# A hybrid decoder block on one core: stores requested by another engine, and the order of retention's statistics

## The chip, the cores and the metric

The kernel runs on one core of a Trainium2 chip. A core has five engines that run side by side, each through its own instructions in order: TensorE (PE: matmuls and transposes), VectorE (DVE), ScalarE (ACT), GpSimd (POOL) and SyncE (SP, which here only requests transfers). Transfers between HBM and the on-chip memory (SBUF) run on 16 DMA engines; a transfer starts when an engine's queue reaches its request, and an engine that requests one waits first, in order, until the data is ready and the place is free. PE's results go to a small memory of banks (PSUM), which ACT and DVE empty. The metric is the device time of one execution in microseconds, the median of several runs.

## The reference

One decoder layer on 1024 tokens of width 1024, in float32:

```python
xn = rmsnorm(x, norm1_g)
qa, ka, va, qr, kr, vr, gr, gate_a, gate_b = split(xn @ w_in)
o_a = mix over 3 dilations of softmax(norm(qa) @ norm(ka).T * s - slope * dist) @ va    # 12 heads of 128
o_r = retention(qr, kr, vr)                       # 4 heads, chunks of 128 tokens, a state of 256 x 512
o_r = head_groupnorm(o_r) * silu(gr)
y = sigmoid(gate_a) * (o_a @ w_proj_a) + sigmoid(gate_b) * (o_r @ w_proj_b)
x = x + y @ w_out
x = x + square(relu(rmsnorm(x, norm2_g) @ w_up)) @ w_down
```

Retention walks through the 8 chunks of a head: each chunk's output is a decayed product inside the chunk plus q times the state, and the state is then decayed and updated with the chunk's k and v. The group norm needs the mean and variance of the 512 outputs of each token and head.

## The kernel before, in words

Every float32 operand is split into a high and a low part (helper `split`, L459 to L466: ACT writes the high part, DVE the low part at L463), and a product is three matmuls of 128x128 by 128x512 (`Pipe.group`, L356). The large products use Strassen's scheme: seven quarter products N1 to N7 for each unit of 256 columns (`product`, L514 and on), whose partial results ACT and DVE combine (L533 to L547). PE's order is written out by hand: `manual_schedule` covers PE, and a `Pipe` drops other matmuls (attention, transposes) between the terms of a product, so many slots later. The other engines' instructions are ordered by a planner, by what its own model expects to be ready, unless the kernel pins one: `tc.keep_in_program_order(ins)` puts `ins` behind the instruction traced before it on the same engine. All pools use `reuse_waits="tile"`: a new tile waits for the tile whose place it takes.

The stages that matter, in order of time:

- **Input projection**, 36 units: 12 of attention's q and k, 8 of retention's output gate gr, 8 of the two mixing gates, 8 of retention's q and k. `result` (L1188) takes each quarter result: a gr quarter goes through sigmoid and a product into a tile `sg` (two buffers) and is stored in `sr_d` (L1206); the others are stored in `sg_d` and `rqk_d` (L1212), from `sg` or straight from the tile `u`.
- **Attention** is woven into the later units (`attend`, L989; `plan_core`). For each head it loads bias, qk, scales and values (L1052 to L1075), scales q and k on DVE (L1069), and works block by block: scores (L1005), exp, transposes (L1016), values (L1026). Two blocks share an `acc` tile of four buffers, which is stored in `acc_d` (L1031); `load_heads` (L581) reads it back to mix the three dilations.
- **Retention**, 4 heads of 8 chunks. `load_chunk` (L1294) brings q, k (L1302) and the silu gate (L1304) two chunks ahead. `decay` makes the inner scores and splits them and q; `output` makes the chunk's product, has ACT copy it (L1364), takes statistics on DVE (L1366, L1367), a power on POOL (L1369) and normalises (L1371); `update` renews the state (L1383); `turn_o` transposes the result (L1396), multiplies by the gate and, for the later half of the chunks, has POOL form the sums of Strassen's scheme (L1410 to L1413), which SP stores in `on_d` (L1391).
- **Projection of attention's output** (pa): 16 products; each is multiplied with a gate on DVE (L1465), put on a list by `leave` and stored in `pa_d` by `send` (L1263).
- **Projection of retention's output** (pb): 8 units in two rounds. A quarter result is gated and added on DVE (L1531); the first round's sums go to `pb_d` and four blocks of the second to `yl_d`, also by `send`. Gates and partial sums come in by `place` (L1250), which loads into the first free buffer of the list `spots`; `send` puts a stored buffer back on that list, and the next load into it waits for the store to land. The operands come from `on_d` (L1276) and are split.

Then follow the output projection, the second norm and the MLP, which the change does not touch. SP requests nearly all transfers of the kernel.

Of the kernel before, what the change touches and what calls it, by code (L numbers as in the profile page):

```python
# [10 lines left out]
F = mybir.dt.float32  # L11
# [6 lines left out]
P = 128  # L18
# [388 lines left out]
def hybrid_block(ctx: ExitStack, tc: tile.TileContext, a: dict, out: bass.AP):  # L407
# [158 lines left out]
    def tokens(rows, g, b):  # L566

        if g == 0:
            return rows[b * P:(b + 2) * P].rearrange("(k p) e -> p k e", k=2)
        if g == 1:  # L570
            return rows.rearrange("(k p r) e -> r p k e", k=2, r=4)[b // 2]
        return rows.rearrange("(p r) e -> p r e", r=8)[:, b:b + 2]
# [416 lines left out]
    def attend(n, b, bias, qk, V, acc, core):  # L989

        slot, g = heads[n]
        h = g * SLOTS + slot
        nk = 2 if has_prev(g, b) else 1
        w = nk * P
        st = {}
        pair, acc = acc, acc[:, b % 2]

        def scores():
            sp = tr.tile([P, 4, P], F, name="tr")[:, :nk].rearrange("p a b -> p (a b)")
            q = qk[b // 4][:, 0, b % 4 * P:b % 4 * P + P]  # L1000
            at = 0
            for c in range((b + 1 - nk) // 4, b // 4 + 1):
                n0, n1 = max(b + 1 - nk, 4 * c), min(b + 1, 4 * c + 4)
                to = slice(at, at + (n1 - n0) * P)
                nc.tensor.matmul(sp[:, to], q, qk[c][:, 1, (n0 - 4 * c) * P:(n1 - 4 * c) * P], start=True, stop=True)  # L1005
                at = to.stop
            s = st["p"] = core.tile([P, 2 * P], F, name="s", bufs=3)
            nc.vector.tensor_tensor_reduce(s[:, :w], sp, bias[:, -w:], op0=OP.add, op1=OP.min,
                                           scale=1.0, scalar=3.0e38, accum_out=acc[:, DH:DH + 1])
            nc.scalar.activation(s[:, :w], s[:, :w], AF.Exp, scale=-1.0, bias=acc[:, DH:DH + 1],  # L1010
                                 accum_out=acc[:, DH + 1:DH + 2])

        def turn(bank):
            tp = bank[:, 1:]
            for j in range(nk):
                nc.tensor.transpose(tp[:, j], st["p"][:, j * P:(j + 1) * P], ident)  # L1016

        def turned(bank):
            st["t"] = core.tile([P, 2, P], F, name="pT", bufs=2)
            nc.scalar.activation(st["t"][:, :nk], bank[:, 1:1 + nk], AF.Copy)  # L1020

        def values(bank):
            po = bank[:, 0]
            for j in range(nk):
                k = b + 1 - nk + j
                nc.tensor.matmul(po, st["t"][:, j], V[k // 2][:, k % 2], start=(j == 0), stop=(j == nk - 1))  # L1026

        def valued(bank):
            nc.scalar.activation(acc[:, :DH], bank[:, 0], AF.Copy)
            if b % 2:  # L1030
                nc.sync.dma_start(tokens(acc_d[:, h, :], g, b - 1), pair)  # L1031

        return scores, turn, turned, values, valued

# [100 lines left out]
    with ExitStack() as ph:  # L1135
# [52 lines left out]
        def result(j, f, cs, src):  # L1188
            if j < NA:
                i = cs.start // 512  # L1190
                r = strides(heads[j][1])
                sg = sgp.tile([P, 512], F, name="sg")
                nc.scalar.activation(sg.rearrange("p (r i) -> p r i", r=r), src.rearrange("p (i r) -> p r i", r=r),
                                     AF.Copy)
                to = qk_d[j, :, f].rearrange("p (r j i) -> j p r i", r=r, j=2)[i]
                src = sg.rearrange("p (r i) -> p r i", r=r)
                nc.sync.dma_start(to, src)
                square(j, f, i, sg)
                return
            n = j - NA  # L1200
            sg = src
            if n < 8:
                sg = sgp.tile([P, 512], F, name="sg")
                nc.scalar.activation(sg, src, AF.Sigmoid)
                nc.vector.tensor_tensor(sg, src, sg, op=OP.mult)
                nc.sync.dma_start(sr_d[2 * n + f, :, cs], sg)  # L1206
                return
            if src.space == PSUM:
                sg = sgp.tile([P, 512], F, name="sg")
                nc.scalar.activation(sg, src, AF.Copy)  # L1210
            n -= 8
            nc.sync.dma_start(sg_d[f, n, :, cs] if n < NG else rqk_d[(n - NG) // 2, (n - NG) % 2, f, :, cs], sg)  # L1212

        unit = {}
        NIN = NA + NG + NQ + 8
# [43 lines left out]
    def send():  # L1259

        while leaving:
            to, y = leaving.pop(0)
            nc.sync.dma_start(to, y)  # L1263
            spots.append(y)

    def sigmoid(x):
# [19 lines left out]
    with ExitStack() as ph:  # L1286
        comb, load = ExitStack(), ExitStack()
        pc = pool(comb, "pc", 2)
        p2 = pool(ret, "p22", 2, "right")
        p2b = pool(ph, "p22b", 2, "right")  # L1290

# [2 lines left out]
        def load_chunk(n):  # L1294

            if n >= RH * NT:
                return
            h, c = divmod(n, NT)
            ts = slice(c * P, (c + 1) * P)
            qk = [p2.tile([P, 2, P], F, name=x, bufs=3) for x in ("rqT", "rkT")]  # L1300
            for i in range(2):
                (nc.scalar if n == 1 else nc.sync).dma_start(qk[i], rqk_d[h, i, :, :, ts].rearrange("f p t -> p f t"))  # L1302
            sr = p2.tile([P, 4, P], F, name="sr", bufs=4)
            nc.sync.dma_start(sr, sr_d[4 * h:4 * h + 4, :, ts].rearrange("f p t -> p f t"))  # L1304
            ready[n] = (*qk, sr)

# [11 lines left out]
        for h in range(RH):  # L1318
# [4 lines left out]
            for c in range(NT):  # L1323
# [9 lines left out]
                def decay(c=c, h=h, it=it, qT=qT, kT=kT):  # L1333
                    sp = ms.tile([P, 512], F, name="ms")
                    for f in range(2):
                        nc.tensor.matmul(sp[:, :P], kT[:, f], qT[:, f], start=(f == 0), stop=(f == 1))  # L1336
                    sm = p2b.tile([P, P], F, name="sm")
                    nc.vector.tensor_tensor(sm, sp[:, :P], maskT[:, h, :], op=OP.mult)
                    it["s"] = p2.tile([P, P], R, name="smh", bufs=3), p2.tile([P, P], R, name="sml", bufs=3)
                    split(*it["s"], sm)  # L1340
                    if c > 0:
                        it["q"] = p2.tile([P, 2, P], R, name="qh", bufs=3), p2.tile([P, 2, P], R, name="ql", bufs=3)
                        split(*it["q"], qT)
                    if c < NT - 1:
                        pt = tr.tile([P, 4, P], F, name="tr")
                        for f in range(2):
                            nc.tensor.transpose(pt[:, f, :], kT[:, f], ident)
                        kzh = p2b.tile([P, 2, P], R, name="kzh", bufs=3)
                        kzl = p2b.tile([P, 2, P], R, name="kzl", bufs=3)
                        nc.scalar.activation(kzh, pt[:, :2], AF.Copy, scale=rc[:, 2, h:h + 1])  # L1350
                        nc.vector.scalar_tensor_tensor(kzl, pt[:, :2], rc[:, 2, h:h + 1], kzh.bitcast(F),
                                                       op0=OP.mult, op1=OP.subtract)
                        it["k"] = kzh, kzl

                def output(c=c, h=h, it=it, state=state):
                    po = ms.tile([P, 512], F, name="ms")
                    terms = [(*it["s"], *it["v"])]
                    if c > 0:
                        for f in range(2):
                            terms.append((it["q"][0][:, f, :], it["q"][1][:, f, :], state["h"][:, f, :],  # L1360
                                          state["l"][:, f, :]))
                    pipe.group(po, terms)
                    on = p2.tile([P, DV], F, name="on")
                    nc.scalar.activation(on, po, AF.Copy)  # L1364
                    st = p2.tile([P, 12], F, name="st")
                    nc.vector.bn_stats(st[:, 0:6], on)  # L1366
                    nc.vector.bn_aggr(st[:, 6:8], st[:, 0:6])  # L1367
                    nc.vector.tensor_scalar(st[:, 8:9], st[:, 7:8], rc[:, 1, h:h + 1], EPS, op0=OP.mult, op1=OP.add)
                    nc.gpsimd.tensor_tensor(st[:, 9:10], st[:, 8:9], half[:, 0:1], op=OP.pow)  # L1369
                    nc.vector.tensor_scalar(st[:, 10:11], st[:, 9:10], rc[:, 0, h:h + 1], None, op0=OP.mult)  # L1370
                    nc.vector.tensor_scalar(on, on, st[:, 6:7], st[:, 10:11], op0=OP.subtract, op1=OP.mult)  # L1371
                    it["o"] = on
# [629 lines left out]
```

## Time and profile before

| | before |
|---|---|
| timed runs, us | 2147.24 median of 3 (2146.48 to 2148.41) |
| the profiled execution, us | 2145.36 |
| its span, first to last instruction, us | 2143.5 |
| PE busy, us | 2132.2 |
| DVE, ACT, POOL busy, us | 1385.2, 1119.1, 312.1 |
| granted TensorE clock | 1.000 |

Rows of the profile name an engine, a line of the kernel (L1031), an operation and its tiles as out<-in. "PEld" is PE's weight load, which overlaps the matmuls; an engine with a q (SPq) is its queue of requests. A row of waits reads: who waited for whom, microseconds in total, how often, the longest. A row of a timeline reads: start, duration, engine, line, operation, and in brackets how long the engine had been idle and what ended that. A row of the chain of waits reads: start, duration, what. Matmuls overlap in this profile, and their ends are modelled.

### The profile page before, as it was taken

Reading aid. Unit: us, or ns where it says so; the run is one execution under the profiler, and the core shown is the slowest. Engines: PE = TensorE matmul, PEld = TensorE weight load, DVE = VectorE, ACT = ScalarE, POOL = GpSimd, SP = SyncE. Lnnn points to the kernel's source line nnn. Section 1 sums busy time; section 2 is a strip of 40 time slices with the busy share of each in tenths; the row PEclk is TensorE's granted clock in tenths of the full one; section 3 lists DMA queues with packets and bytes.
Section 4 is the critical chain, followed back from the end, with each engine's and each line's share of the span. In section 5 each row is a group of like instructions: output and inputs, shape, how many; then the busy total and the mean of one; then the engine's idle time right before and its main releaser. Section 6 shows DMA issues by size and latency. Waiting matters only on the chain.

```text
span 2143.5 us, 28506 instructions
## 1 busy us (share of the span) xinstructions
PE 2132.2 (99%) x9840; PEld 1752.5 (82%) x9840; DVE 1385.2 (65%) x2360; ACT 1119.1 (52%) x2154; POOL 312.1 (15%) x340
## 2 busy tenths in 40 slices
PE   9999999999999999999999999999999999999999
PEld 7887777888888888888888887888788888888887
DVE  7944434656556565657767777973865557788884
ACT  8534555434655454445545655542655555755552
POOL 1000000000000000003123110000000000777773
PEclk9999999999999999999999999999999999999999
DMA  9433333333667766765364498854354556645443
GB/s 331 152 113 98 108 104 103 104 134 134 194 197 216 210 197 192 221 192 163 104 177 128 150 307 294 305 196 142 105 168 140 159 157 200 217 156 195 155 143 108
DMA packets 297489, 368.24 MB, mean 172 GB/s; under 512 B 35249, under 2 KB 202609, under 8 KB 297089
## 3 DMA queue, kind: packets, MB, share of 16 engines
q1 hardware_dynamic: 296800, 366.16, 53.7%
q8 instruction: 77, 1.26, 0.3%
q14 instruction: 68, 0.55, 0.1%
q10 hardware_dynamic: 544, 0.26, 0.0%
HBM read 249.76 MB, written 116.59 MB: 171 GB/s over the span
## 4 chain that ended last, share of the span: by engine, by line
PE 89%; DVE 4%; DMA 2%; issue 2%; ACT 2%; POOL 1%; SPq 0%; POOLq 0%; DVEq 0%; ACTq 0%
PE mm L356 45%; PE ms L356 34%; PE ms L811 3%; PE tr L1026 1%; PE tr L1005 1%; PE mm L811 1%; DVE wl L463 1%; PE tr L1016 1%; PE tr L1396 1%; PE tr L1158 1%; PE ms L1336 1%; ACT wh L460 1%; DVE xl L463 1%; DVE raw L160 1%; DVE xn L1682 0%
## 5 line engine op out<-in xcount | busy, mean ns | idle before, releaser
L463 DVE TENSOR_TENSOR wl<-raw,wh 128x1024 fp32r<-128x1024 f32 (+1 forms) x301 | 333.7, 1110 | 388.9 <-ACT wh L460 387.8
L460 ACT ACTIVATE wh<-raw 128x1024 fp32r<-128x1024 f32 (+1 forms) x301 | 288.0, 959 | 290.5 <-PE ms L356 96.0
L356 PE MATMUL mm<-xh,wh 128*128 128x512 f32 x960 | 387.7, 404 | 0.6 <-ACT q L1718 0.4
L356 PE MATMUL mm<-xh,wl 128*128 128x512 f32 x960 | 374.9, 391 | 0.5 <-DVE wl L463 0.5
L356 PE MATMUL mm<-xl,wh 128*128 128x512 f32 x960 | 374.1, 390 | 0.3 <-DVE xl L463 0.3
L356 PE MATMUL ms<-xh,wh 128*128 128x512 f32 x784 | 317.6, 405 | 1.5 <-ACT u L541 1.5
L356 PE MATMUL ms<-xh,wl 128*128 128x512 f32 x784 | 306.2, 391 | 0.1
L356 PE MATMUL ms<-xl,wh 128*128 128x512 f32 x784 | 305.5, 390 | 0.0
L356 PEld LDWEIGHTS mm<-xh,wl 128*128 128x128 f32 x960 | 180.2, 188 | 40.0 <-DVE wl L463 1.2
L356 PEld LDWEIGHTS mm<-xh,wh 128*128 128x128 f32 x960 | 180.5, 188 | 35.4 <-ACT q L1718 0.8
L356 PEld LDWEIGHTS mm<-xl,wh 128*128 128x128 f32 x960 | 180.7, 188 | 34.8 <-DVE xl L463 0.7
L356 PE MATMUL mm<-wh,xh 128*128 128x512 f32 x474 | 192.1, 405 | 0.0
L356 PE MATMUL mm<-wh,xl 128*128 128x512 f32 x474 | 185.6, 392 | 0.0
L356 PE MATMUL mm<-wl,xh 128*128 128x512 f32 x474 | 184.7, 390 | 0.0
L356 PEld LDWEIGHTS ms<-xh,wh 128*128 128x128 f32 x784 | 147.4, 188 | 40.7 <-issue 10.1
L1369 POOL TENSOR_TENSOR st<-st,half 128x1 f32<-128x1 f32 x32 | 25.2, 788 | 1043.8 <-DMA at<-acc_d 886.5
L356 PEld LDWEIGHTS ms<-xh,wl 128*128 128x128 f32 x784 | 147.1, 188 | 32.3 <-DVE wl L463 0.5
L356 PEld LDWEIGHTS ms<-xl,wh 128*128 128x128 f32 x784 | 147.6, 188 | 27.3
L356 PEld LDWEIGHTS mm<-wh,xl 128*128 128x128 f32 x474 | 89.0, 188 | 19.8
L356 PEld LDWEIGHTS mm<-wl,xh 128*128 128x128 f32 x474 | 89.4, 189 | 16.3
L356 PEld LDWEIGHTS mm<-wh,xh 128*128 128x128 f32 x474 | 89.2, 188 | 16.2 <-ACT ms L1809 0.3
L160 DVE TENSOR_TENSOR raw<-raw 128x512 f32<-128x512 f32 x120 | 83.5, 696 | 1.9
(368 smaller groups left out, 3836.7 us busy)
## 6 DMA issues: line engine op xcount, KB each, us to landing
raw<-in_w_up SPq DMA_DIRECT2D x32, 512.0 KB
h_d<-s SPq DMA_DIRECT2D x64, 256.0 KB
raw<-in_w_down SPq DMA_DIRECT2D x30, 512.0 KB
xl<-on_d SPq DMA_DIRECT2D x28, 512.0 KB
raw<-in_w_aqk_q SPq DMA_DIRECT2D x24, 512.0 KB
qk_d<-sg SPq DMA_DIRECT2D x48, 256.0 KB
qk<-qk_d SPq DMA_DIRECT2D x24, 512.0 KB
rb<-rs_d SPq DMA_DIRECT2D x24, 512.0 KB
```

The source lines that it names most:

```text
L160: ins = self.nc.vector.tensor_tensor(x, x, y, op=OP.add)
L356: self.nc.tensor.matmul(ps, x, y, start=start, stop=stop, skip_group_check=not first)
L460: hi = nc.scalar.activation(dst_h, src, AF.Copy)
L463: lo = nc.vector.tensor_tensor(dst_l, src, dst_h.bitcast(F), op=OP.subtract)
L811: nc.tensor.matmul(pm, x, w, start=k == m == 0, stop=k == n - 1 and m == 2)
L1005: nc.tensor.matmul(sp[:, to], q, qk[c][:, 1, (n0 - 4 * c) * P:(n1 - 4 * c) * P], start=True, stop=True)
L1016: nc.tensor.transpose(tp[:, j], st["p"][:, j * P:(j + 1) * P], ident)
L1026: nc.tensor.matmul(po, st["t"][:, j], V[k // 2][:, k % 2], start=(j == 0), stop=(j == nk - 1))
L1158: nc.tensor.matmul(to[m:m + 32], pick[:, 31 - n:63 - n], x, start=n == 0, stop=n == HEADS - 1)
L1336: nc.tensor.matmul(sp[:, :P], kT[:, f], qT[:, f], start=(f == 0), stop=(f == 1))
L1369: nc.gpsimd.tensor_tensor(st[:, 9:10], st[:, 8:9], half[:, 0:1], op=OP.pow)
L1396: nc.tensor.transpose(pt[:, f, :], it["o"][:, f * P:(f + 1) * P], ident)
```

## The change

Four requests move from SP's queue to POOL's: the stores of the silu gates, of the mixing gates and retention's q and k (`result`), of attention's pairs (`valued`), and of the gated blocks (`send`). In retention the tiles of q, k and the silu gate get a pool of their own, opened ahead of the pool they were in, with the same number of buffers. The low part of q's split is pinned behind the DVE instruction traced before it, and so are the two statistics instructions.

```diff
         def valued(bank):
             nc.scalar.activation(acc[:, :DH], bank[:, 0], AF.Copy)
             if b % 2:
-                nc.sync.dma_start(tokens(acc_d[:, h, :], g, b - 1), pair)
+                nc.gpsimd.dma_start(tokens(acc_d[:, h, :], g, b - 1), pair)
...
-                nc.sync.dma_start(sr_d[2 * n + f, :, cs], sg)
+                nc.gpsimd.dma_start(sr_d[2 * n + f, :, cs], sg)
                 return
...
-            nc.sync.dma_start(sg_d[f, n, :, cs] if n < NG else rqk_d[(n - NG) // 2, (n - NG) % 2, f, :, cs], sg)
+            nc.gpsimd.dma_start(sg_d[f, n, :, cs] if n < NG else rqk_d[(n - NG) // 2, (n - NG) % 2, f, :, cs], sg)
...
         while leaving:
             to, y = leaving.pop(0)
-            nc.sync.dma_start(to, y)
+            nc.gpsimd.dma_start(to, y)
             spots.append(y)
...
         pc = pool(comb, "pc", 2)
+        p2a = pool(ret, "p22a", 3, "right")
         p2 = pool(ret, "p22", 2, "right")
...
-            qk = [p2.tile([P, 2, P], F, name=x, bufs=3) for x in ("rqT", "rkT")]
+            qk = [p2a.tile([P, 2, P], F, name=x) for x in ("rqT", "rkT")]
...
-            sr = p2.tile([P, 4, P], F, name="sr", bufs=4)
+            sr = p2a.tile([P, 4, P], F, name="sr", bufs=4)
...
-                        split(*it["q"], qT)
+                        split(*it["q"], qT, False, True)
...
-                    nc.vector.bn_stats(st[:, 0:6], on)
-                    nc.vector.bn_aggr(st[:, 6:8], st[:, 0:6])
+                    tc.keep_in_program_order(nc.vector.bn_stats(st[:, 0:6], on))
+                    tc.keep_in_program_order(nc.vector.bn_aggr(st[:, 6:8], st[:, 0:6]))
```

## The prediction

> **What bounds the kernel now.** I read the page first, then the stages, then what TensorE (PE) waits for, then the queue of SyncE (SP).
>
> ```profile
> span 2143.5 us, 28506 instructions
> ...
> PE 2132.2 (99%) x9840; PEld 1752.5 (82%) x9840; DVE 1385.2 (65%) x2360; ACT 1119.1 (52%) x2154; POOL 312.1 (15%) x340
> ```
>
> PE is busy in all but 11.3 us of the span (2143.5 - 2132.2). No store costs anything unless it makes PE late. The change touches five stages, in this order: the silu gates of the input projection; its last part with attention woven in; retention; the projection of attention's output (pa); the projection of retention's output (pb). Columns: span, then busy time of PE, PEld, DVE, ACT, POOL, granted clock, DMA share, GB/s.
>
> ```profile
> 360.00:546.00 186.00, 185.67 (x834) 151.54 (x833) 108.86 (x155) 91.80 (x139) 0.00 (x0) 1.00 0.39 130
> 546.00:913.00 367.00, 366.65 (x1874) 309.71 (x1873) 218.69 (x608) 187.10 (x525) 0.00 (x0) 1.00 0.66 203
> 913.00:1232.00 319.00, 317.63 (x1539) 262.71 (x1538) 229.12 (x518) 171.88 (x360) 67.28 (x84) 1.00 0.53 153
> 1232.00:1286.00 54.00, 53.95 (x240) 43.55 (x239) 39.95 (x57) 30.98 (x47) 9.11 (x13) 1.00 0.92 309
> 1286.00:1440.00 154.00, 152.23 (x668) 124.69 (x667) 129.59 (x172) 82.19 (x116) 0.00 (x0) 1.00 0.78 267
> ```
>
> Span less PE: 0.33 + 0.35 us in the two parts of the projection, 1.37 in retention, 0.05 in pa, 1.77 in pb; 3.87 us in all. The clock is 1.00 throughout, so throttling plays no part. GpSimd (POOL) does nothing at all in the projection and in most of pa and pb. PE's waits between 500 and 1400 us, with total, number and longest:
>
> ```profile
> PE ms L356 <- ACT u L541: 1.5, 2, 1.0
> PE tr L1396 <- DVE on L1371: 1.1, 3, 0.6
> PE tr L1005 <- DVE acc L1008: 0.4, 1, 0.4
> PE tr L1005 <- DVE qk L1069: 0.3, 1, 0.3
> ```
>
> Idle time understates a wait, because matmuls overlap. The rows around the longest one, in pb:
>
> ```profile
> 1320.67 0.39 PE L356 MATMUL mm<-xl,wh 128*128 128x512 f32 x1
> 1320.90 0.39 PE L356 MATMUL mm<-xh,wl 128*128 128x512 f32 x1
> 1322.30 0.50 PE L356 MATMUL ms<-xh,wh 128*128 128x512 f32 x1 [1.01 <-ACT u L541]
> ```
>
> Matmuls start 0.23 us apart, but each is shown for 0.39. The wait reads 1.01 us, and the start came 1.40 - 0.23 = 1.17 us late: 0.16 is hidden under each wait. I estimate ten waits in these stages (seven in the rows above, and shorter ones for the 0.57 us of idle time that these leave), so the change can return at most 3.87 + 10 x 0.16, about 5.4 us: about 1.0 in the projection, 2.1 in retention, 2.3 in pb. That is 0.25% of the kernel, the ceiling of what it aims at.
>
> **The moved stores, on SP's side.** By the loops, 180 requests change queue: 32 silu gates, 32 gates, 32 retention q and k, 48 attention pairs, 16 + 16 + 4 gated blocks. What SP loses in cost and in waits:
>
> ```profile
> L1206 SPq DMA_DIRECT2D sr_d<-sg x32: 319/326/877, 362.8 to 546.1; - x32
> ```
> ```profile
> SPq L1031 <- ACT acc L1029: 64.7, 24, 5.7
> ...
> SPq L1263 <- DVE s L1531: 21.7, 17, 3.4
> ```
>
> At the median 0.326 us, 180 requests are 59 us of SP's time, and the stores of pairs and blocks held SP another 64.7 + 21.7 = 86.4 us while it waited for ACT and DVE. Loads stand behind those waits. Only two places show PE paying for it. In attention:
>
> ```profile
> 822.94 0.37 SPq L1031 DMA_DIRECT2D acc_d<-acc  x1
> 823.40 0.53 SPq L1059 DMA_DIRECT2D qk<-qk_d  x1
> 824.03 0.55 SPq L1061 DMA_DIRECT2D rb<-rs_d  x1
> ```
> ```profile
> 830.65 0.75 DVE L1069 SCALAR_TENSOR_TENSOR qk<-qk,gqk,rb 128x512 f32<-128x512 f32 x1 [2.92 <-DMA rb<-rs_d]
> ```
>
> The loads of the next head leave right behind a pair's store; DVE then sits 2.92 us for them and PE is late for the score matmul behind it (the 0.4 row; 0.56 with the hidden part). Freed of the store, the loads can leave earlier, and 0.6 us is enough. The other wait of L1005 (0.3) has DVE's own queue ahead of it and may stay. I take -0.6; bounds 0 and -1.0.
>
> In pb:
>
> ```profile
> 1312.77 0.32 SPq L1263 DMA_DIRECT2D pb_d<-s  x1
> 1313.13 0.94 SPq L1276 DMA_DIRECT2D xl<-on_d  x2
> ```
> ```profile
> 1320.19 1.06 ACT L460 ACTIVATE xh<-xl 128x1024 fp32r<-128x1024 f32 x1 [0.38 <-DMA xl<-on_d]
> ```
>
> Two loads of 512 KB leave right after a store that waited for DVE; ACT, in order, waits for their landing (1320.19), evacuates u after it, and that is the 1.01 us above. Leaving 1.2 us earlier would erase it, if the DMA engines were free; at a share of 0.78 they are partly not. I take half of the 2.3: -1.2; bounds 0 and -2.3.
>
> **The same stores, on POOL's side.** No row shows a DMA request by POOL. From below a request costs SP's 0.326 us, from above POOL's longest neighbour here:
>
> ```profile
> 985.70 1.60 POOL L1411 TENSOR_TENSOR n<-onT,onE 128x256 f32<-128x256 f32 x1
> ```
>
> I take 1.0, nearer the middle since nothing tells: 180 us of an engine that is idle there, so 0 on the path. What covers it is the slack of the buffers. A gate's store is watched by the next user of its buffer:
>
> ```profile
> 438.99 0.93 SPq L1206 DMA_DIRECT2D sr_d<-sg  x2
> ...
> 441.37 0.60 ACT L1204 ACTIVATE sg<-ms 128x512 f32<-128x512 f32 x1 [0.70 <-DMA sr_d<-sg]
> ```
>
> It landed 2.4 us after its issue. With 1.0 more, ACT waits 1.7 instead of 0.7; ACT is busy 91.80 of 186 us there and PE idles 0.33, so this is paid from slack. A pair has four buffers, and its readers come slots later. New in-order waits on POOL: at the start of pa, a gated block's store that waits for DVE can stand ahead of the last chunk's power (L1369); ahead of the first chunk's, only the last retention k. I price both at 0.
>
> [...]
>
> **Retention's statistics and chunks.** PE's wait for L1371 comes at the change of heads:
>
> ```profile
> 985.07 1.64 DVE L463 TENSOR_TENSOR wl<-raw,wh 128x1024 fp32r<-128x1024 f32 x1 [0.26 <-ACT wh L460]
> 986.63 0.95 DVE L463 TENSOR_TENSOR ql<-rqT,qh 128x256 fp32r<-128x256 f32 x1
> 987.50 0.68 DVE L1366 BATCH_NORM_STATS2 st<-on 128x6 f32<-128x512 f32 x1
> 988.11 0.67 DVE L1383 SCALAR_TENSOR_TENSOR St<-St,ms 128x512 f32<-128x512 f32 x1
> 988.70 0.17 DVE L1367 BATCH_NORM_AGGREGATE st<-st 128x2 f32<-128x6 f32 x1
> ```
>
> A state update of 0.67 stands between the two statistics, and ql of 0.95 just ahead of them. With the statistics together, the aggregate comes some 0.5 us earlier (988.70 - 987.50 - 0.68), and POOL's power and the normalisation follow. If ql has gone before, another 0.9. Each of the three waits loses about 0.37 + 0.16 = 0.53 on average: the first two should vanish, the longest (0.6) shrink. I take -1.1; bounds 0 (a pin says only "not before", and the planner may leave the order) and -1.6. What is late next is the state, 0.2 us later; its matmuls come a slot after and show no wait. The chunks' own pool moves buffers, not work: the first chunk's loads may find their place free sooner or later, and PE's loss there is among the short waits above, 0.57 us with all others. I take -0.1; bounds -0.5 and +0.5.
>
> **Sum.** -0.6 - 1.2 + 0 - 1.1 - 0.1 = -3.0 us. The profiled execution took 2145.36 us (span 2143.5 and 1.86 around it) and would take 2142.4. The three timed runs have their median 1.88 above it, so the prediction is 2147.24 - 3.0 = 2144.2. Its own range, by the bounds, is 2142.0 (the ceiling of 5.4) to 2147.6.
>
> **The rivals.** First, slower: the stores land later, in pb. Its buffers (spots) go from a store to the next load, which waits on SP for the landing:
>
> ```profile
> 1328.06 4.60 DMA pb_d<-s
> 1332.73 5.22 DMA s<-sg_d
> ```
>
> Landing of the store, landing of the load, then a sigmoid in ACT's queue ahead of u: this chain already sets the pace there. The row of ACT's waits for such a load:
>
> ```profile
> ACT s L1267 <- DMA s<-sg_d: 7.8, 4, 3.2
> ```
>
> I take it that these four rounds reach PE. If a store lands d later, pb pays 4d and gains nothing, the other terms (-1.8) stay: slower from d = 0.45 us, by more than 4.3 us from 1.5. At d = 2 it is 2147.24 - 1.8 + 8 = 2153.4. For it speaks that landing already takes 4.60 against 2.4 on idle engines; against it, that a queue of its own need not stand behind SP's loads. [...]
>
> Second: POOL and DVE slow each other.
>
> ```profile
> L463 DVE TENSOR_TENSOR wl<-raw,wh 128x1024 fp32r<-128x1024 f32 (+1 forms) x301 | 333.7, 1110 | 388.9 <-ACT wh L460 387.8
> ```
>
> While L1411 ran its 1.60, the wl of DVE took 1.64, against a mean of 1.11 for its group. Were DVE held 0.5 us by each of some 20 stores in pb, it would have 10 us more on 129.59 of 154; half of it ahead of an evacuation is +5, so 2147.2 - 1.8 + 5 = 2150.4. Against it: L1411 reads two operands, a request reads none that the trace shows.
>
> Third: the change doesn't bring what it says. The planner orders anew, pins hold nothing forward, and as many small waits come as go: about 2147. For it speaks that the waits are 0.2 to 1.2 us and any reordering moves them.
>
> Fourth: freer SP also relieves waits later than 1440 us, where a part of the other 11.3 - 3.87 = 7.4 us lies; with the ceiling and another 1: 2141.
>
> **How the numbers follow.** Forecast 0.52, late landing 0.17, contention 0.06, nothing 0.15, more 0.10. About 0.2%, or 4.3 us, is what a measurement can tell from no change: below 2142.9 is faster, above 2151.5 slower. Faster: a quarter of the forecast (0.13) and the fourth, 0.23. Slower: the first rival and half the second, 0.20. The rest, 0.57, is no change. The range, 2140.5 to 2151.5, leaves out most of the first rival and little else.
>
> **What would show it.** Right: no acc store ahead of L1061; L1366 and L1367 adjacent; PE's waits for L1371 under 0.6 us in all, for L541 under 1; the projection still without PE idle; POOL requests under 1.6 us. Wrong: ACT waiting for sr_d much longer than 0.70, or for s<-sg_d longer than 7.8 in all; wl rows of 1.6 us beside POOL's requests; PE idle in 1286 to 1440 above 1.77.

## The result, and the profile after

The changed kernel took 2162.7 us (median of 5 runs, 2157.64 to 2163.7) against 2148.12 (2146.48 to 2149.49, 5 runs) for the kernel before on the same chip: a ratio of 1.0065, with a 95% interval of 1.0054 to 1.0075. It is slower; a gain of 3.0 us had been forecast, too small to be told from no change. The profiled execution took 2157.64 us. It is the fastest of the five, 5 us below their median, so its trace shows less of the loss than most. The page of the changed kernel:

```profile
span 2155.8 us, 28596 instructions
...
PE 2134.5 (99%) x9840; PEld 1754.3 (81%) x9840; DVE 1380.6 (64%) x2360; ACT 1119.9 (52%) x2154; POOL 416.9 (19%) x520
```

The span grew by 12.3 us (2155.8 - 2143.5). PE's idle time grew by 10.0 of them (2155.8 - 2134.5 = 21.3, from 11.3), and its busy time by 2.3, though its work is the same 9840 instructions. The stages, with the columns of the prediction (span, then PE, PEld, DVE, ACT, POOL, granted clock, DMA share, GB/s):

```profile
360.00:546.00 186.00, 185.66 (x834) 151.60 (x834) 108.14 (x154) 90.73 (x136) 18.03 (x33) 1.00 0.39 130
546.00:913.00 367.00, 367.00 (x1877) 310.37 (x1876) 218.80 (x609) 190.21 (x528) 67.50 (x108) 1.00 0.64 206
913.00:1232.00 319.00, 318.48 (x1545) 263.71 (x1544) 228.05 (x523) 171.57 (x361) 70.58 (x92) 1.00 0.51 151
1232.00:1286.00 54.00, 49.61 (x218) 39.37 (x216) 31.69 (x45) 26.66 (x42) 14.77 (x24) 1.00 0.89 299
1286.00:1440.00 154.00, 146.18 (x627) 119.47 (x628) 123.94 (x165) 80.53 (x115) 11.37 (x21) 0.97 0.75 252
```

Span less PE, before to after: attention 0.35 to 0.00, retention 1.37 to 0.52, pa 0.05 to 4.39, pb 1.77 to 7.82. Attention and retention idle less, as the prediction had it; the experiments will tell which of the two gains stays. pa and pb lost 10.4 us, and in pb the granted clock fell to 0.97. PE's waits, by the line that it waited for:

```profile
PE mm L356 <- ACT ms L533: 6.3, 2, 6.1
PE ms L356 <- ACT u L541: 3.4, 2, 2.7
PE ms L356 <- DVE s L1466: 2.0, 2, 1.1
PE tr L1397 <- DVE on L1372: 0.5, 2, 0.3
...
PE tr L1005 <- DVE qk L1069: 0.3, 1, 0.3
```

The largest is one wait of 6.1 us at the border of pa and pb. It can be followed back. ACT's timeline there:

```profile
1277.78 1.06 ACT L460 ACTIVATE xh<-xl 128x1024 fp32r<-128x1024 f32 x1 [8.07 <-DMA xl<-on_d]
...
1289.17 0.58 ACT L533 ACTIVATE ms<-mm 128x512 f32<-128x512 f32 x1
```

ACT stood 8.07 us at the split of an operand, then worked off what had gathered behind it, and the copy of N1 that PE waited for (`ms`, L533) came last. The operand was requested late. SP's timeline:

```profile
1259.37 0.38 SPq L1276 DMA_DIRECT2D xl<-on_d  x1
1266.41 0.33 SPq L1250 DMA_DIRECT2D s<-sg_d  x1
...
1270.63 0.33 SPq L1250 DMA_DIRECT2D s<-pa_d  x1
1271.01 0.51 SPq L1276 DMA_DIRECT2D xl<-on_d  x1
```

Between 1259.7 and 1266.4 SP stood at a gate's load whose place still had to be stored, and again until 1270.63; the operand (L1276, 1271.01) stood behind both. By this chain the first rival of the prediction, late landing of the stores, seemed to have won. The experiments say otherwise.

### The profile page after: what moved, and what is told of

The parts are those of the page before. It is cut to its first block, busy times and chain, and to the rows that moved or that the text cites. A ratio compares the mean times of both kernels' runs of the same rounds, so it can differ in the third digit from the quotient of the medians.

```text
span 2155.8 us, 28596 instructions
## 1 busy us (share of the span) xinstructions
PE 2134.5 (99%) x9840; PEld 1754.3 (81%) x9840; DVE 1380.6 (64%) x2360; ACT 1119.9 (52%) x2154; POOL 416.9 (19%) x520
## 4 chain that ended last, share of the span: by engine, by line
PE 83%; issue 7%; DVE 4%; POOL 2%; ACT 2%; DMA 1%; SPq 0%; POOLq 0%; DVEq 0%; ACTq 0%
PE mm L356 42%; PE ms L356 30%; PE ms L811 3%; PE tr L1026 1%; PE tr L1005 1%; PE mm L811 1%; DVE wl L463 1%; PE tr L1016 1%; ACT wh L460 1%; DVE xl L463 1%; PE tr L1397 1%; PE tr L1158 1%; DVE raw L160 1%; PE ms L1337 1%; DVE xn L1683 0%
## 5 line engine op out<-in xcount | busy, mean ns | idle before, releaser
L463 DVE TENSOR_TENSOR wl<-raw,wh 128x1024 fp32r<-128x1024 f32 (+1 forms) x301 | 333.1, 1108 | 402.5 <-ACT wh L460 401.4
L1206 POOL DMA_DIRECT2D sr_d<-sg x32 | 17.5, 548 | 463.1 <-DVE sg L1205 457.5
L1785 POOL TENSOR_TENSOR rl<-xh,rh 128x256 fp32r<-128x256 f32 x31 | 31.4, 1025 | 286.2 <-ACT rh L1784 286.1
```

Source lines behind the costliest of these rows:

```text
L463: lo = nc.vector.tensor_tensor(dst_l, src, dst_h.bitcast(F), op=OP.subtract)
L1785: nc.gpsimd.tensor_tensor(l, src, h.bitcast(F), op=OP.subtract)
```

## Experiments: which part costs

First, which edit. The kernel in which only `send` goes back to SP:

```diff
-            nc.gpsimd.dma_start(to, y)
+            nc.sync.dma_start(to, y)
             spots.append(y)
```

> The changed kernel with one line back: the gated blocks' stores (send, L1263) are requested by SP again; gates, pairs and retention stay changed. Theory T: the whole loss comes from send's stores, whose late landing holds the loads that reuse their buffers in pa and pb; what is left of the change gains the idle time that PE lost in attention (0.35 us) and retention (0.85 us). So 0.6 to 2 us under the kernel before, about 2146.9, PE idle under 0.5 us in pa and under 2.5 in pb. Rival R (any request on POOL costs, by contention with DVE or by reordering): still 5 us or more above the kernel before, since 144 of the 180 requests stay on POOL. Rival P (retention's new pool and pins shift what follows): still about 2160, PE idle 4 us in pa.

Measured: 2147.3 us against 2149.03 for the kernel before, ratio 0.9993 (0.9984 to 1.0002). This is what theory T asked for, and rivals R and P did not.

The converse, the kernel before with the same line alone changed:

```diff
-            nc.sync.dma_start(to, y)
+            nc.gpsimd.dma_start(to, y)
             spots.append(y)
```

> The kernel before with send's 36 stores alone requested by POOL. Theory T: the loss of the change and a little more, since the small gains are missing: 2158 to 2165, PE idle about 4 us in pa and 8 in pb. In the compiled order ACT still splits one half of N6's operand behind both halves of N4's, where the changed kernel has two halves behind one of N4's; if that order is what costs, pa loses less than in the changed kernel. Rivals R and P: at most a quarter of the loss, 2148 to 2152.

Measured: 2165.67 against 2149.03, ratio 1.0080 (1.0066 to 1.0094): the whole loss, at the upper end of theory T.

Retention's part alone, all stores on SP:

```diff
+        p2a = pool(ret, "p22a", 3, "right")
...
-                        split(*it["q"], qT)
+                        split(*it["q"], qT, False, True)
...
+                    tc.keep_in_program_order(nc.vector.bn_stats(st[:, 0:6], on))
+                    tc.keep_in_program_order(nc.vector.bn_aggr(st[:, 6:8], st[:, 0:6]))
```

> The kernel before with retention's part alone: the chunks' pool and the three pins, all stores on SP. Theory T: PE idle in retention falls from 1.37 to about 0.5, so 0.9 to 1.3 us faster: about 2147.0, which the interval may not tell from no change. Rival P: slower by 5 us or more, with the loss at the end of retention and in pa.

Measured: 2147.97 against 2149.03, ratio 0.9994 (0.9985 to 1.0003).

Gates and attention's pairs alone, nothing else changed against the kernel before:

```diff
+                nc.gpsimd.dma_start(tokens(acc_d[:, h, :], g, b - 1), pair)
...
+                nc.gpsimd.dma_start(sr_d[2 * n + f, :, cs], sg)
...
+            nc.gpsimd.dma_start(sg_d[f, n, :, cs] if n < NG else rqk_d[(n - NG) // 2, (n - NG) % 2, f, :, cs], sg)
```

> The kernel before with the stores of gates and of attention's pairs alone requested by POOL. Theory T: between 0 and 0.8 us faster (PE idle 0.35 to 0 in the part with attention): about 2147.7, no change to the measurement. Rival R: 144 requests of 0.55 to 0.72 us beside DVE cost 2 us or more, 2150 and up, with PE idle between 360 and 913 us.

Measured: 2147.44 against 2149.03, ratio 0.9995 (0.9986 to 1.0003). Theory T holds: 36 stores of `send` carry the whole loss, and the other 144 moved requests cost nothing that can be measured. The stage of attention in the fourth and in the third kernel:

```profile
546.00:913.00 367.00, 367.00 (x1877) 310.27 (x1876) 219.36 (x609) 190.47 (x529) 67.24 (x107) 1.00 0.64 203
```
```profile
546.00:913.00 367.00, 364.41 (x1860) 307.00 (x1859) 218.37 (x608) 186.49 (x523) 0.00 (x0) 1.00 0.67 204
```

The pairs' stores on POOL leave PE no idle time in attention here. The second row is a warning: in the retention kernel attention has 2.59 us of idle time instead of 0.35, though no line of that stage was edited. Nor had the order there changed: by line and tile, ACT, DVE and SP go through the stage as before, up to SP's last requests in it, and both waits of PE (1.4 and 1.2 us) lie ahead of these. One wait, PE's for the acc tile of L1008 near 832 us, reads 0.35, 0.93 and 1.40 us in the traces of three kernels with this same order (before, `send` alone, retention alone). So a difference of a microsecond or two in the idle time of a single trace says little.

## Experiments: why `send` costs

Four attempts on single suspects, all of them edits of the changed kernel. The loads into the same buffers go to POOL as well (in `place`):

```diff
-        nc.sync.dma_start(spots[0], src)
+        nc.gpsimd.dma_start(spots[0], src)
```

> The changed kernel with the loads of gates and partial sums into the same buffers (place, L1250) requested by POOL as well, so that a load waits for its buffer's store on POOL and no operand or weight load of SP stands behind that wait. Theory H (what costs is SP standing at a place whose store has not landed, 30.7 us for pa_d and 31.5 for pb_d against 7.1 and 6.7 before, with operand loads in order behind it): most of the loss returns, 2146 to 2152, and PE idles under 4 us in pa and pb together against 12.2. Rival L (the late landing itself: gate, sigmoid and ACT's queue behind it): still 2157 or more, since a load waits for the same landing. Rival O (ACT's new order of the operand splits, which stays much as in the changed kernel): still 2157 or more, with ACT waiting for an operand of N4 in pa.

Measured: 2167.29 against 2146.81, ratio 1.0100 (1.0082 to 1.0118). POOL's waits:

```profile
POOL s L1250 <- DMA pa_d<-s: 45.6, 13, 6.3
POOL s L1250 <- DMA pb_d<-s: 41.4, 15, 6.3
```

SP no longer stood at these loads, and POOL stood instead; nothing was won, where theory H had asked for 2152 or less. The splits of the operands pinned in program order:

```diff
-            split(xh, xl, xl.bitcast(F), upto < len(work))
+            split(xh, xl, xl.bitcast(F), True)
```

> The changed kernel with every split of pb's operands pinned in program order on ACT, so that N4's halves come again behind both halves of N2 and N6; all stores as changed. Rival O: the loss of pa and of the gap at the start of pb returns: PE idle in pa under 1 us, the 6.1 us wait of PE for ms L533 gone, 2150 to 2154. Theory H and rival L: the gate loads stand and land as late as in the changed kernel, so at most 3 us return: 2158 to 2163.

Measured: 2166.72 against 2146.81, ratio 1.0095 (1.0075 to 1.0115). The wait of 6.1 us for L533 was gone, as rival O had it, but the time was not (2150 to 2154 were expected): the pins hold pb's splits too, and new waits stood in their place:

```profile
PE mm L356 <- DVE xl L463: 3.0, 2, 1.7
PE ms L356 <- ACT xh L460: 2.5, 2, 1.3
PE mm L356 <- ACT wh L460: 2.3, 1, 2.3
```

pa's stores alone on POOL:

```diff
-    def send():
+    def send(by=None):
...
-            nc.gpsimd.dma_start(to, y)
+            (by or nc.sync).dma_start(to, y)
...
-            send()
+            send(nc.gpsimd)
             leave(pa_d[d, :, cs], gates[n])
```

> The changed kernel with the stores of pb (pb_d, yl_d) back on SP; those of pa stay on POOL. If pa and the operands split during it carry the larger part (the 6.2 us gap at the start of pb follows an operand that was requested in pa): 2154 to 2159. If pb's chain from store to load to sigmoid is the larger part, as the first rival of the prediction had it: 2149 to 2152.

Measured: 2155.47 against 2146.81, ratio 1.0041 (1.0026 to 1.0056). pb's alone, with the argument in the other place:

```diff
             fetch(n + 2)
-            send()
+            send(nc.gpsimd)
```

> The changed kernel with pa's stores back on SP; those of pb stay on POOL. ACT's compiled order of splits in pa is that of the kernel before. If pa carries the larger part: 2149 to 2153, PE idle in pa near 0.1 us, the wait for u L541 of 2.7 us stays. By the first rival of the prediction, whose place was pb alone: 2154 to 2160.

Measured: 2153.66, ratio 1.0030 (1.0018 to 1.0041). So the two stages lose about 8.7 and 6.9 us (2155.47 and 2153.66 less 2146.81), neither much more than the other, and about the whole together. The second lies above what was expected if pa carried the larger part, and just below what the first rival would give. The prediction's first rival knew of pb only.

None of these four tells cause from cause, for one reason: whatever is edited, the planner orders ACT, DVE and SP anew. The compiled order of ACT's splits around the border of pa and pb shows it (a and b are the halves of an operand):

```
before, and send on SP     N1a N1b N2a N2b N6a N6b N4a N4b
changed kernel             N1a N1b N2a N4a N2b N6a N4b N6b
send alone on POOL         N1a N1b N2a N2b N6a N4a N4b N6b
```

The operand at which ACT stood 8.07 us is the first half of N4, which the planner had put fourth instead of seventh. (One half of N3, which the changed kernel has in between, is left out.) By the lists of pa and pb that the next kernels hold, at least 18 of ACT's 201 instructions, 9 of DVE's 226 and 24 of SP's 211 have to change place to turn the order of the kernel with `send` on SP into that of the changed kernel. So the next four kernels hold the order and change the queue, or hold the queue and change the order. The edges below are meant to set the order of issue alone, with no wait for completion:

```diff
+def _follow(tc, nc, orders):
+    traced = nc.cur_bb.bb.instructions
+    how = mybir.DependencyInfo(mybir.DependencyClass.NoSync, mybir.DependencyReason.DATA)
+    for places in orders:
+        mine = [traced[int(k)] for k in places.split()]
+        for a, b in zip(mine, mine[1:]):
+            tc.add_manual_dep(b, a.name, how, reason="order")
...
+    _follow(tc, nc, (ACT_ORDER, DVE_ORDER,))
```

A list names the instructions of pa and pb of one engine in the order that another kernel gave them. Stores on POOL, ACT and DVE in the order of the kernel with `send` on SP:

> The changed kernel, all stores on POOL, but ACT's 201 and DVE's 226 instructions of pa and pb are held, by issue-order edges alone, in the order that they have in the kernel with send on SP (2147.3). SP's order of loads stays much as in the changed kernel. Theory O (what costs is the order that the planner gives ACT and DVE when the stores leave SP: a sigmoid or a split put ahead of evacuations that PE needs, its load not landed yet): 2146 to 2151. Rival B (SP, no longer held by stores that wait for DVE, requests the loads in another order and in bursts that the DMA engines can't serve): 2155 or more. Rival L (a store requested by POOL lands later): 2155 or more.

Measured: 2157.41 against 2147.71, ratio 1.0044 (1.0031 to 1.0057). SP's requests, left to the planner, stand in this trace as in the changed kernel's but for two. Stores on POOL, and ACT, DVE and SP in that order:

```diff
-    _follow(tc, nc, (ACT_ORDER, DVE_ORDER,))
+    _follow(tc, nc, (ACT_ORDER, DVE_ORDER, SP_ORDER,))
```

> As the last, and SP's 211 loads and other requests of pa and pb are held in the order of the kernel with send on SP too, so that only the queue that requests the 36 stores differs from it. Theory O: 2146 to 2150, as the last. Rival B in its first form (the order of the loads): 2146 to 2150 here, but 2155 or more in the last. Rival B in its second form (loads are no longer paced by the stores between them) and rival L: 2153 or more.

Measured: 2148.32 against 2147.71, ratio 1.0002 (0.9993 to 1.0010). Stores on SP, ACT and DVE in the order of the changed kernel (the lists hold that order here):

```diff
-            nc.gpsimd.dma_start(to, y)
+            nc.sync.dma_start(to, y)
...
+    _follow(tc, nc, (ACT_ORDER, DVE_ORDER,))
```

> The converse: the kernel with send back on SP, but ACT and DVE held in pa and pb in the order that they have in the changed kernel. No store is on POOL there beyond gates and pairs. Theory O: 2153 to 2163, with ACT waiting for operands and gates as in the changed kernel and PE idle 6 us or more in pa and pb together. Rivals B and L: 2146 to 2150.

Measured: 2166.99 against 2147.71, ratio 1.0091 (1.0078 to 1.0105). Stores on SP, and ACT, DVE and SP's loads in the order of the changed kernel, that is, the last kernel with a third list:

```diff
-    _follow(tc, nc, (ACT_ORDER, DVE_ORDER,))
+    _follow(tc, nc, (ACT_ORDER, DVE_ORDER, SP_ORDER,))
```

> The converse with SP's loads too: send on SP, and ACT, DVE and SP's loads of pa and pb held in the order of the changed kernel, the stores between them where the planner puts them. Theory O: as the last, 2153 to 2163. Rival B in its first form: 2153 or more here, and 2146 to 2150 in the last. Rival L: 2146 to 2150 in both.

Measured: 2158.94 against 2147.71 (2157.44 to 2165.99 in 5 runs), ratio 1.0050 (1.0036 to 1.0064).

The second and the fourth settle it. By line and tile, ACT, DVE and SP of the second kernel go through the whole trace in the order of the kernel with `send` on SP, and those of the fourth in the order of the changed kernel, the stores of `send` apart. With every order held, moving 36 stores to POOL costs nothing that can be measured. With every store on SP, the changed kernel's orders alone cost 11.2 us (2158.94 - 2147.71) of the change's 14.6. The two intervals overlap (1.0036 to 1.0064, 1.0054 to 1.0075), so whether the remaining 3.4 us are anything is not shown. PE's idle time in pa and pb comes to 12.2 us in the trace of the fourth kernel (1.02 + 11.20) as in that of the changed one (4.39 + 7.82), though this trace is of the slowest of its five runs:

```profile
1232.00:1286.00 54.00, 52.98 (x237) 42.71 (x236) 30.27 (x47) 24.15 (x42) 10.45 (x14) 1.00 0.92 307
1286.00:1440.00 154.00, 142.80 (x605) 115.84 (x604) 124.72 (x164) 82.15 (x117) 0.00 (x0) 0.96 0.77 256
```

Rival L is out, and rival B in its second form. Theory O and rival B in its first form are each a part of the answer. The first and the second kernel differ in SP's order alone, and that is 9.1 us (2157.41 - 2148.32). ACT's and DVE's order, with SP's left to the planner, costs 19 (third kernel); SP's order there is neither of the two, so this is not the price of ACT's and DVE's alone. The orders belong together: the changed ones on all three engines cost less than ACT's and DVE's without SP's. In that third kernel ACT's waits are:

```profile
ACT xh L460 <- DMA xl<-on_d: 23.0, 6, 13.1
ACT s L1267 <- DMA s<-sg_d: 19.8, 5, 7.5
```

ACT splits N4 early there while SP loads it late: 13.1 us in one wait. SP's waits for a store's landing in pa and pb, in four kernels in turn: before, changed, all orders held with the stores on POOL, and `send` on SP:

```profile
SPq L1250 <- DMA pa_d<-s: 7.1, 4, 2.6
...
SPq L1250 <- DMA pb_d<-s: 6.7, 4, 4.3
```
```profile
SPq L1250 <- DMA pb_d<-s: 31.5, 13, 5.1
SPq L1250 <- DMA pa_d<-s: 30.7, 10, 6.6
```
```profile
SPq L1250 <- DMA pb_d<-s: 22.4, 9, 5.0
SPq L1250 <- DMA pa_d<-s: 19.3, 8, 6.0
```
```profile
SPq L1250 <- DMA pa_d<-s: 7.4, 5, 2.3
SPq L1250 <- DMA pb_d<-s: 7.3, 6, 4.3
```

The third pair is the one to keep in mind: 41.7 us of SP standing at places not yet stored, against 13.8 before, and the kernel is as fast as before. SP standing is what one sees in the slow kernel, but in this order little that PE needs stands behind it. The stages pa and pb of that kernel:

```profile
1232.00:1286.00 54.00, 52.16 (x230) 41.79 (x229) 37.97 (x52) 30.92 (x47) 15.85 (x26) 1.00 0.89 295
1286.00:1440.00 154.00, 151.27 (x659) 124.34 (x658) 127.94 (x170) 81.68 (x116) 10.87 (x20) 0.99 0.78 264
```

And of the kernel with `send` on SP:

```profile
1232.00:1286.00 54.00, 53.47 (x238) 43.51 (x238) 39.48 (x54) 31.03 (x47) 7.96 (x11) 1.00 0.90 304
1286.00:1440.00 154.00, 151.11 (x662) 123.54 (x661) 128.54 (x171) 81.63 (x116) 0.00 (x0) 1.00 0.80 265
```

PE idles 1.84 and 2.73 us in the first, 0.53 and 2.89 in the second: some 1.2 us more, which may be the price of POOL's queue itself. Neither the timed runs nor these two traces can tell it from nothing, since one order gave waits a microsecond apart above.

What stays open: why the planner chose these orders is not seen in any trace. That it counted on the loads to land earlier than they did fits ACT's waits for them, and is not shown. Nor was each engine tried alone: ACT's order was never held without DVE's, and SP's old order with ACT's and DVE's new one was not tried.

## Why the prediction was wrong

**Its forecast, 2144.2, missed by 18.5 us, and its range ended at 2151.5.** The step that failed is the costing of the stores "on POOL's side" at "0 on the path", together with the third rival's "as many small waits come as go". Taken as the price of a queue, the 0 was right (2148.32 with the orders held). But the sum treated the order of all other instructions as given, and in this kernel it isn't: PE's order is written out, that of ACT, DVE and SP is planned anew. The new orders alone cost 11.2 of the 14.6 us (2158.94 with every store of `send` on SP). The third rival named the mechanism and put a mean of nothing on it, from waits of 0.2 to 1.2 us. In pa and pb, where the DMA share is 0.75 to 0.92 and ACT goes in order, waits are longer: behind one split that had moved from seventh to fourth place, the trace of the changed kernel has PE wait 6.1 us. No run moved that split alone.

**The request by POOL, 1.0.** The prediction took 1.0 us, between 0.326 and 1.60. All requests by POOL in the changed kernel lie between two groups of its page:

```profile
L1031 POOL DMA_DIRECT2D acc_d<-acc x48 | 34.5, 719 | 179.0 <-ACT acc L1029 177.9 <-issue 0.9
...
L1263 POOL DMA_DIRECT2D yl_d<-s x4 | 2.2, 541 | 37.2 <-DVE s L1532 37.2
```

0.54 to 0.72 us: inside the bounds, and too high by 0.3 to 0.5.

**The landing, +1.0 and the first rival.** Median times from issue to landing, changed kernel:

```profile
sr_d<-sg POOLq DMA_DIRECT2D x32, 256.0 KB, 2.3
...
pa_d<-s POOLq DMA_DIRECT2D x16, 256.0 KB, 4.2
pb_d<-s POOLq DMA_DIRECT2D x16, 256.0 KB, 3.9
```

The silu gate's store landed after 2.3 us, where the prediction had read 2.4 for SP and added 1.0. For pa, a store of the kernel before and the load that waited for it:

```profile
1271.30 0.32 SPq L1263 DMA_DIRECT2D pa_d<-s  x1
...
1275.88 0.32 SPq L1250 DMA_DIRECT2D s<-pa_d  x1
```

That is at most 4.6 us for SP, and the prediction's row for pb was 4.60; few landings of SP's stores can be read, and POOL's medians of 4.2 and 3.9 lie near them. The prediction set this 4.60 against 2.4 "on idle engines", but the DMA engines were not idle then: before the change their share was 0.92 during the 2.4 (438.99 to 441.40 us) and 0.87 during the 4.60 (1328.06 to 1332.66 us). What rules the first rival out is the kernel with all orders held. Its pb stores land later than the changed kernel's, and it is as fast as the kernel before:

```profile
pb_d<-s POOLq DMA_DIRECT2D x16, 256.0 KB, 5.1
```

One sign that the prediction had named for this rival did come: ACT waited 14.1 us for gates in pa and pb (s<-sg_d) instead of 7.8. But this wait goes with the order and not with the queue: it is 12.5 with the changed orders and the stores on SP, and 4.1 with the old orders and the stores on POOL. The rival's sign was right, its cause was not, and 2153.4 was near the pb kernel (2153.66) by chance.

**Attention, -0.6.** The idle time went from 0.35 to 0.00 and the row "PE tr L1005 <- DVE acc L1008: 0.4" is gone; the wait for qk of 0.3 stayed, as said. That this is the change's doing is not shown: the kernel with `send` on SP, in which attention is edited alike, has the wait for acc back at 0.5 and idles 0.45 us in this stage. The reason is no surer: no acc store stands ahead of L1061 on SP any more, yet DVE's longest wait for rb is 3.0 us in the changed kernel against 2.9 before.

**pb, -1.2, bounds 0 and -2.3.** Wrong in sign: +6.05 us of idle time. The two loads did lose the store ahead of them, and the earlier request was taken as a gain. But SP's requests then left in another order, and that order alone cost 9.1 us.

**Retention, -1.1.** The idle time fell by 0.85, and PE's waits for L1371 (now L1372) from 1.1 to 0.5 us, as called. This gain stays: 0.45 to 1.02 us of idle time in every trace with the edit, 1.16 to 1.40 in those without it. Half of the reason was wrong: the state update (now L1384) still stands between the two statistics in 22 of 32 chunks, as before. What vanished is the 0.95 of ql, which stood right ahead of them in 26 chunks before and stands there in none now. The three waits before were not at the changes of heads either, but at the sixth chunk of the first three heads. DVE's waits for ACT's copy, before and after, show how:

```profile
DVE st L1366 <- ACT on L1364: 4.5, 5, 1.5
```
```profile
DVE st L1367 <- ACT on L1365: 38.1, 27, 2.6
```

DVE now waits for the copy, 27 times, with the pinned statistics at its head, so nothing long gets ahead of them. The prediction's third rival had said that "pins hold nothing forward"; in an engine that goes in order, one can.

**The chunks' pool, -0.1.** Not told apart from the pins; with them 2147.97 against 2149.03, no change to the measurement.

**The second rival, contention.** Out: 144 requests on POOL beside DVE give 2147.44 against 2149.03, the 36 of pa and pb with the orders held 2148.32 against 2147.71. DVE's splits (L463) take 1108 ns on average in the changed kernel, 1110 before.

**The sums.** The bounds of the terms add up to 2141.8 and 2147.7, where the prediction wrote 2142.0 and 2147.6, and four landings of 1.5 us less 1.8 are 4.2, not 4.3. Nothing rests on the difference.

## What to carry to other kernels

Where a planner orders the engines, moving one request edits the order of all of them; a sum over the moved instructions then prices only a part of the change. Here the other part was the larger by far, in stages whose DMA engines were busy for 0.75 to 0.92 of the time. Compare the compiled orders before reading waits as causes, and hold them (one run with the old orders and the new queue, one with the new orders and the old queue) before believing a mechanism that the trace suggests. The part of this change worth keeping is everything but `send`, and even that is within the noise: 0.9993 (0.9984 to 1.0002).

## What the runs showed of the hardware that was not expected

PE paid twice for its waits. The timeline of PE in the changed kernel, and its clock in two stretches:

```profile
1289.80 0.79 PE L356 MATMUL mm<-xh,wh 128*128 128x512 f32 x1 [6.05 <-ACT ms L533]
1290.39 0.63 PE L356 MATMUL mm<-xl,wh 128*128 128x512 f32 x1
1290.82 0.63 PE L356 MATMUL mm<-xh,wl 128*128 128x512 f32 x1
```
```profile
1288.00:1293.00 5.00, 3.20 (x8) 2.53 (x9) 5.00 (x7) 3.70 (x6) 0.17 (x1) 0.51 0.97 312
1293.00:1298.00 5.00, 5.00 (x24) 4.10 (x23) 3.00 (x4) 2.65 (x4) 0.54 (x1) 1.00 0.96 370
```

After 6.05 us of idle time the granted clock was 0.51 (1288 to 1293 us), and the matmuls started 0.43 us apart instead of 0.23. From 1292.94 us, 3.1 us after the first of them, they stood 0.23 apart again, and the clock of the next stretch was 1.00. A shorter wait in pb did the same:

```profile
1371.90 0.80 PE L356 MATMUL ms<-xh,wh 128*128 128x512 f32 x1 [2.71 <-ACT u L541]
```
```profile
1370.00:1375.00 5.00, 3.10 (x8) 2.51 (x9) 3.57 (x5) 4.70 (x7) 0.00 (x0) 0.66 0.98 381
```

In pa and pb of the changed kernel 11 steps are of this length, 6 behind the first wait and 5 behind the second: 11 x 0.20 = 2.2 us, of the 2.3 by which PE's busy time grew. After the 11.1 us wait of the kernel with the stores on SP and ACT's and DVE's changed order the clock was 0.50 too (1294 to 1298 us).

The length of one gap does not decide alone. One of 2.66 us in the kernel with all orders held was followed by a clock of 0.66 over 5 us, one of 2.76 in the kernel with ACT's and DVE's order held by no loss at all:

```profile
1325.00:1330.00 5.00, 5.00 (x16) 3.96 (x16) 4.93 (x7) 5.00 (x8) 0.54 (x1) 0.66 0.77 249
```
```profile
1373.00:1377.00 4.00, 4.00 (x18) 3.31 (x19) 3.96 (x6) 4.00 (x6) 0.00 (x0) 1.00 1.03 390
```

In the kernel with the loads on POOL a gap of 2.31 us was enough (0.57 in 1260 to 1264 us). So for gaps of 2.31, 2.66, 2.71, 6.05 and 11.1 us the clock read 0.50 to 0.66 in a stretch of 4 or 5 us that holds their end or lies just behind it, and for one of 2.76 us it read 1.00. What besides its length makes a gap cost the clock, these traces do not show.
